# A three-part reordering in a one-core encoder layer: gates' chain, weight sums of the up-projection, places for the down weights

## The chip, the core and the metric

The kernel runs on one core of a Trainium2 chip. Its engines work side by side, each through its own row of instructions in a fixed order, and wait for one another by semaphores: TensorE does the matrix products (PE in the profile; its weight loads are PEld), VectorE (DVE) and ScalarE (ACT) the elementwise work, GpSimd (POOL) some sums, and SyncE (SP) issues most DMAs. The metric is the device time of one execution in microseconds (us); lower is better. TensorE's clock has two levels, 1.2 and 2.4 GHz, and the profile shows which of them was granted as a share of the full one.

## The reference, cut to what matters

One encoder layer over 1024 tokens of width 1024: a token mixer (a bidirectional mLSTM group and a neighbourhood attention group), cross-attention into 256 memory tokens, and a gated convolutional feed-forward block. The parts that the change touches are the mLSTM's gates and the two projections of the feed-forward block.

```python
# mLSTM, per chunk of 128 tokens: lfc = log_sigmoid(forget gate), ic = input gate
a = jnp.cumsum(lfc, axis=-1)
d_log = jnp.where(tril, a[..., :, None] - a[..., None, :] + ic[..., None, :], -jnp.inf)
m_t = jnp.maximum(a + m[..., None], jnp.max(d_log, axis=-1))
m_new = jnp.maximum(a_end + m, jnp.max(a_end[..., None] - a + ic, axis=-1))

# feed-forward: D_FF = 2816, so w_up is 1024 x 5632 and w_down 2816 x 1024
h = x @ w_up + b_up
h = lax.conv_general_dilated(h, w_dw[:, None, :], ...) + b_dw
g, u = jnp.split(h, 2, axis=-1)
y = jax.nn.gelu(g, approximate=False) * u
return y @ w_down + b_down
```

## The kernel before

All large products work on numbers split into a high and a low f16 half: ACT makes the high half (L204), DVE the low half (L205), and PE does three products for each (high by high L225, high by low L226, low by high L227). A split cannot start before its float32 source, the raw weights, has come by DMA, and it needs a place to write to. Places are rings: `wraw` has two raw places, `whi`/`wlo` five places each, `ur` two. Who asks for a place waits until the reader of its last holder is done.

The program is written in the order of the loops below, but a scheduler at build time sets each engine's final row, by its own estimate of times; generators (`next(...)`) and `issue_after` hints place the work of one stage between the products of another.

*Gates.* While the token columns are projected in four column blocks c of eight token tiles tt (the loop at L808, PE's `tk` products), the gates' chain `gate_gen` (L358) runs in six steps, each called by `next(gg)` at L835: the logarithms; the cumulative sums on PE (L376 to L378); a transpose of `g_sb` (L386) and 14 steps of a cumulative maximum on DVE (L394, L395, seven for each direction, alternating between two buffers `cx`) with the copies to `gm` (L399, L400); a product that turns the maxima into a row (L403) and the recursion over the chunks (L414, L416); the broadcast of it (L419 to L421); the last transpose (L432). Between them the splits of the next block's weights (`wlo<-wr`), copies out of PE's banks (`ev` L814, `stage` L205), statistics (`mx` L183, `l` L311) and, on POOL, sums for operands T (`tsum`, turned to f16 at L743) share DVE and POOL.

*Up-projection.* The work is divided into 22 units of w_up, and in each the 2x2 blocks of weights (A) and tokens (B) go through Winograd's form of Strassen's product: seven products with sums S1 to S4 of the weight blocks and T1 to T4 of the token blocks. `to_B` (L1315) turns a token tile into B, and every second one also makes its T sums on DVE (L1342 to L1345), in two `wraw` places, and splits them (ACT L1348, DVE or POOL L1349; `TX1l` and `TX1h` hold T). `Units.prep` makes a unit's S sums on POOL (L1505 to L1508), also in two `wraw` places, and then splits them on ACT and DVE. `units.load` (L1464) fetches a unit's raw weights into the `ur` ring, `units.bound` (L1471) takes their sum of absolutes, and `units.scale` a power of two from the maximum that PE's `mx` (L183) spreads. The start of it is written at L1524 to L1559. Before, `next(prep1)` (the S sums of the second unit) and `units.bound(2)` stood ahead of the loop that does the first products of both units and, in it, the last `to_B`.

*Down-projection.* The 1024 output columns are two halves c of 512, and the 22 rows of blocks f are in six groups j (four blocks in each, two in the last). `w_pair(j, c)` (L1650) loads and splits one such group. The first half runs over j outside and tiles tt inside (L1754), then over the last group j = 5 (L1771); the second half runs over the tiles (L1790), with j = 5 first and then j = 0 to 4. So the second half's first product needs the pair (5,1), and its first tile needs all six. Pair (5,1) has a place of its own in `yp`, before and after; before, all others used the `whi`/`wlo` ring, which still holds the first half's groups. Lines L1758 and L1774 copy and add the first half's results out of PE's banks (`half`).

Of the kernel before, what the change touches and what calls it, by code (L numbers as in the profile page):

```python
# [8 lines left out]
F32 = mybir.dt.float32  # L9
# [47 lines left out]
def encoder(ctx, tc, I, out):  # L57
# [21 lines left out]
    def bank(name):  # L79
        key = "mem" if name == "tk" else name  # L80
        turn[key] = turn.get(key, -1) + 1
        tag = SET[name][turn[key] % len(SET[name])]
        return pp.tile([128, 512], F32, name=name, tag=tag, bufs=NB[tag])
# [198 lines left out]
    with ExitStack() as ca:  # L282

        yml = None
        with ExitStack() as cm:
# [254 lines left out]
            with ExitStack() as c2:  # L540
# [257 lines left out]
                with ExitStack() as c1:  # L798
# [7 lines left out]
                    for c in range(4):  # L806
                        w, ic = cw[2 + c]
                        for tt in range(NT):  # L808
# [6 lines left out]
                            j = slice(c % 2 * 256, c % 2 * 256 + 256)  # L815
# [15 lines left out]
                                    next(cu0)  # L831
                            if c == 2 and tt == 4:
                                next(cu0)
                            if c < 2 and tt % 2 == 0:
                                next(gg, None)  # L835
                            if tt % 2:
                                with tc.issue_after(d.ins):
# [386 lines left out]
    with ExitStack() as cb_:  # L1224
# [3 lines left out]
        f16 = lambda t: t.bitcast(F16)  # L1228
# [210 lines left out]
        ur = cb_.enter_context(tc.tile_pool(name="unitraw", bufs=1, reuse_waits="tile"))  # L1439
# [104 lines left out]
        run(prep0)  # L1544
        units.load(2)
        next(o7)
        next(prep1)
        units.bound(2)

        with rtx:  # L1550

            X, Z, W = {}, {}, {}
            for v in range(2):
                X[v], Z[v] = bank("z"), bank("z")
                prod(X[v], v, "A11", "B11", True, False)
                if rq and v == 1:
                    to_B(*rq.pop(0))
                prod(Z[v], v, "A12", "B21", True, True)
                W[v] = bank("z")  # L1559

# [3 lines left out]
        with ExitStack() as cE:  # L1566
# [83 lines left out]
            def w_pair(j, c):  # L1650

                n = min(4, NFF - 4 * j)
                if j == 5 and c == 1:
                    h, l = yhome[5][:, 2, 0], yhome[5][:, 2, 1]
                else:
                    h, l = (wp.tile([128, 2048], F16, name=t, tag=t, bufs=5) for t in ("whi", "wlo"))
                for i in range(n // 2):
# [82 lines left out]
        with ExitStack() as cF:  # L1740
# [13 lines left out]
            for j in range(1, 5):  # L1754
                for tt in range(NT):
# [10 lines left out]
                        V.tensor_scalar(ratio, sy[1][0], s1, 2.0 ** -14, op0=OP.mult, op1=OP.mult)  # L1766
                    if j == 4 and tt == 0:
                        y_pair(NG, sy[1][1])
                    if j == 4 and tt in (4, 6):
                        w_pair((tt - 4) // 2, 1)  # L1770
            for tt in range(NT):  # L1771
                p2 = bank("dn")
                dmm(p2, tt, 0, range(NG, NFF), True, True)
                V.scalar_tensor_tensor(half0[:, tt], p2, ratio, half0[:, tt], op0=OP.mult, op1=OP.add)  # L1774
                if tt in (1, 3, 5):
                    w_pair(2 + tt // 2, 1)
            w_pair(5, 1)
            lb = yhome[5][:, 3].rearrange("p n t -> p (n t)").bitcast(F32)
            S.dma_start(lb, bcast_row(I["ln3_b"], D))
            rs = {}  # L1780
# [113 lines left out]
```

## Time and profile before

| | us |
|---|---|
| median of 3 runs | 1557.06 (1556.63 to 1559.12) |
| profiled execution, own time | 1562.55 |
| its span, first to last instruction | 1560.8 |
| PE busy in the span | 1476.6 (95%) |
| DVE, ACT, POOL busy | 1045.2, 807.2, 573.3 |
| mean granted clock of PE | 0.977 of full |

A row of a timeline gives the start and the length of an instruction (or of several in a run, with xN), and in square brackets how long its engine had been idle and what ended that. "dn<-whi,yp" reads: the instruction writes the tile dn and reads whi and yp. `z` are the up-projection's banks, `dn` the down-projection's, `tk` and `mem` those of the token projection. `yp` holds y (the input of the down-projection) in its halves. A step that PE waits for is found by its releaser; that one has a row on its own engine, with its own wait.

### The profile page before, as it was taken

The page shows a single profiled execution, that of the slowest core. Times are in us where ns is not written, and L with a number is a line of the kernel's source. Part 1 is how long each engine was busy: PE and PEld are TensorE (multiplying, and loading weights), DVE is VectorE, ACT ScalarE, POOL GpSimd, SP SyncE. Part 2 cuts the span into 40 slices and gives each one's busy share as a digit, 9 for nine tenths or more (in the row PEclk, how much of TensorE's full clock was granted, in tenths as well). Part 3 has the DMA queues.
Part 4 walks back from the last instruction along what each step waited for, and adds up shares of the span by engine and source line. Part 5 has one row for each costly group of instructions (what it writes and reads, how often), then busy time and mean ns, then how long its engine had stood idle before and what let it go on. Part 6 is the DMA issues. An engine that isn't in the chain of part 4 may idle for free.

```text
span 1560.8 us, 21755 instructions
## 1 busy us (share of the span) xinstructions
PE 1476.6 (95%) x8134; PEld 879.3 (56%) x8134; DVE 1045.2 (67%) x1961; ACT 807.2 (52%) x1367; POOL 573.3 (37%) x446
## 2 busy tenths in 40 slices
PE   7899899999999999999999979999999999997998
PEld 6788787456765888864555434444444444443443
DVE  7876756535667778575356768888888877925333
ACT  5444554655553666433344668777777756611000
POOL 6243265502324766043112364444444410301342
PEclk9999899999999999999999989999999999998999
DMA  8833564314644732653011332223223424832111
GB/s 297 323 139 122 173 204 157 111 48 130 162 136 149 229 125 82 243 189 122 28 41 41 122 138 109 108 108 116 114 109 122 169 87 157 296 112 69 41 68 54
DMA packets 84896, 208.62 MB, mean 134 GB/s; under 512 B 7091, under 2 KB 36019, under 8 KB 81462
## 3 DMA queue, kind: packets, MB, share of 16 engines
q1 hardware_dynamic: 84496, 206.46, 38.1%
q8 instruction: 64, 1.05, 0.3%
q0 software_dynamic: 144, 0.49, 0.2%
q14 instruction: 42, 0.34, 0.1%
q10 hardware_dynamic: 150, 0.27, 0.0%
HBM read 158.34 MB, written 49.35 MB: 133 GB/s over the span
## 4 chain that ended last, share of the span: by engine, by line
PE 52%; DVE 22%; DMA 9%; ACT 9%; issue 4%; POOL 4%; SPq 1%; DVEq 0%; ACTq 0%; POOLq 0%
PE dn L226 5%; PE dn L227 5%; PE dn L225 5%; PE S L225 3%; PE S L227 3%; PE S L226 3%; DMA sv<-in_w_down_dram 3%; DVE wlo L205 3%; DVE cbuf L1587 3%; DVE cbuf L1588 2%; PE z L226 2%; PE z L225 2%; PE z L227 2%; PE cl L225 2%; PE cl L226 2%
## 5 line engine op out<-in xcount | busy, mean ns | idle before, releaser
L225 PE MATMUL dn<-whi,yp 128*128 128x512 f16 x336 | 127.4, 382 | 1.4 <-ACT whi L204 1.4
L226 PE MATMUL dn<-wlo,yp 128*128 128x512 f16 x336 | 128.1, 382 | 0.0
L227 PE MATMUL dn<-whi,yp 128*128 128x512 f16 x336 | 127.9, 381 | 0.0
L1505 POOL TENSOR_TENSOR wraw<-ur 128x512 f32<-128x512 f32 x22 | 44.0, 2000 | 200.5 <-issue 186.4
L1587 DVE SCALAR_TENSOR_TENSOR cbuf<-C,wdw,cbuf 128x1024 f32<-128x1024 f32 x44 | 75.8, 1722 | 28.3 <-ACT cbuf L1586 28.2
L225 PEld LDWEIGHTS <-whi 128*128 128x128 f16 x540 | 53.6, 99 | 62.0 <-issue 9.5
L227 PEld LDWEIGHTS <-wlo 128*128 128x128 f16 x540 | 53.7, 99 | 59.6 <-DVE wlo L205 3.6
L226 PEld LDWEIGHTS <-whi 128*128 128x128 f16 x540 | 53.6, 99 | 57.3 <-issue 4.1
L205 DVE SCALAR_TENSOR_TENSOR wlo<-wraw,us,whi 128x1024 f16<-128x1024 f32 (+1 forms) x48 | 67.6, 1425 | 17.7 <-ACT whi L204 17.4
L253 ACT ACTIVATE r<-r,lnrs 128x1024 f32<-128x1024 f32 x19 | 23.6, 1243 | 99.6 <-DVE lnrs L252 99.6
L1588 DVE SCALAR_TENSOR_TENSOR cbuf<-C,wdw,cbuf 128x1024 f32<-128x1024 f32 x44 | 70.5, 1602 | 1.2
L225 PEld LDWEIGHTS <-yp 128*128 128x128 f16 x352 | 34.6, 98 | 51.9 <-issue 11.1
L204 ACT ACTIVATE whi<-wraw,us 128x1024 f16<-128x1024 f32 (+1 forms) x48 | 51.3, 1103 | 17.5 <-DVE us L177 11.3
L1586 ACT ACTIVATE cbuf<-C,bdw,wdw 128x1024 f32<-128x1024 f32 x44 | 54.5, 1238 | 10.6 <-DVE C L1623 9.8
L243 POOL TENSOR_TENSOR lnrs<-lnrs,mhalf 128x1 f32<-128x1 f32 x32 | 19.7, 616 | 105.6 <-DVE lnrs L242 90.2
L227 PEld LDWEIGHTS <-yp 128*128 128x128 f16 x352 | 34.7, 98 | 42.2 <-issue 1.1
L226 PEld LDWEIGHTS <-yp 128*128 128x128 f16 x352 | 34.6, 98 | 42.0 <-issue 1.1
L225 PE MATMUL tk<-whi,Be 128*128 128x256 f16 (+1 forms) x192 | 54.1, 282 | 1.4 <-ACT whi L204 1.4
L227 PE MATMUL tk<-whi,Be 128*128 128x256 f16 (+1 forms) x192 | 53.7, 280 | 0.0
L226 PE MATMUL tk<-wlo,Be 128*128 128x256 f16 (+1 forms) x192 | 53.6, 279 | 0.0
L225 PE MATMUL tk<-whi,Bo 128*128 128x256 f16 (+1 forms) x192 | 52.9, 275 | 0.0
L1182 ACT ACTIVATE P<-P,mn 128x256 f32<-128x256 f32 (+1 forms) x64 | 35.6, 557 | 33.3 <-DVE mn L1180 33.1
(496 smaller groups left out, 4863.2 us busy)
## 6 DMA issues: line engine op xcount, KB each, us to landing
ur<-in_w_up_dram SPq DMA_DIRECT2D x22, 1024.0 KB
sv<-in_w_down_dram SPq DMA_DIRECT2D x22, 512.0 KB
y<-cbuf SPq DMA_DIRECT2D x22, 512.0 KB
ur<-y SPq DMA_DIRECT2D x11, 1024.0 KB
wraw<-in_w_down_dram SPq DMA_DIRECT2D x22, 512.0 KB
r<-h SPq DMA_DIRECT2D x19, 512.0 KB
h<-r SPq DMA_DIRECT2D x16, 512.0 KB
wraw<-in_w_tok_dram SPq DMA_DIRECT2D x10, 512.0 KB
```

Source lines behind the costliest of these rows:

```text
L204: A.activation(hi, src, AF.Copy, scale=s)
L205: return V.scalar_tensor_tensor(lo, src, s, hi, op0=OP.mult, op1=OP.subtract)
L225: T.matmul(ps, lh, rh, start=first, stop=False, skip_group_check=skip)
L226: T.matmul(ps, lh, rl, start=False, stop=False, skip_group_check=skip)
L227: return T.matmul(ps, ll, rh, start=False, stop=last, skip_group_check=skip)
L243: G.tensor_tensor(rs[:, 0:1], rs[:, 0:1], mhalf[:, 0:1], OP.pow)
L253: A.activation(r, r, AF.Identity, scale=rs[:, 0:1], bias=rs[:, 1:2])
L1182: A.activation(P[:, :nk], P[:, :nk], AF.Exp, scale=-1.0, bias=mn[:, 0:1], accum_out=mn[:, 1:2])
L1505: G.tensor_tensor(S1, A21, A22, OP.add)
L1586: A.activation(c, C[:, 1:SEQ + 1], AF.Identity, scale=wdw[:, 1, j:j + 1], bias=bdw[:, j:j + 1])
L1587: V.scalar_tensor_tensor(c, C[:, 0:SEQ], wdw[:, 0, j:j + 1], c, op0=OP.mult, op1=OP.add)
L1588: V.scalar_tensor_tensor(c, C[:, 2:SEQ + 2], wdw[:, 2, j:j + 1], c, op0=OP.mult, op1=OP.add)
```

## The change

1. The gates' chain takes a step at every third tile, n = 8c + tt = 1, 4, 7, 10, 13, 16, where it took one at every second, n = 0, 2, 4, 6, 8, 10.
2. `next(prep1)` and `units.bound(2)` move behind the loop with the first products, so the last tile's `to_B` with its T sums comes ahead of the second unit's S sums.
3. The second half's down weights (3,1) and (4,1) go to places in the `ur` ring, each tile holding both halves. The pairs are called in the order (5,1), (0,1), (1,1), (2,1) at tt = 1, 3, 5, 7 of j = 4, and (3,1), (4,1) at tt = 0, 2 of the loop over the last group. Before, it was (0,1), (1,1) at tt = 4, 6 of j = 4, then (2,1), (3,1), (4,1) at tt = 1, 3, 5 of the next loop, and (5,1) behind it.

```diff
--- before.py
+++ after.py
@@ -831,7 +831,7 @@
                                     next(cu0)
                             if c == 2 and tt == 4:
                                 next(cu0)
-                            if c < 2 and tt % 2 == 0:
+                            if (8 * c + tt) % 3 == 1 and 8 * c + tt < 17:
                                 next(gg, None)
                             if tt % 2:
                                 with tc.issue_after(d.ins):
@@ -1544,8 +1544,6 @@
         run(prep0)
         units.load(2)
         next(o7)
-        next(prep1)
-        units.bound(2)
 
         with rtx:
 
@@ -1557,6 +1555,8 @@
                     to_B(*rq.pop(0))
                 prod(Z[v], v, "A12", "B21", True, True)
                 W[v] = bank("z")
+            next(prep1)
+            units.bound(2)
 
 
 
@@ -1652,6 +1652,9 @@
                 n = min(4, NFF - 4 * j)
                 if j == 5 and c == 1:
                     h, l = yhome[5][:, 2, 0], yhome[5][:, 2, 1]
+                elif j > 2 and c == 1:
+                    t = f16(ur.tile([128, 2048], F32, name="ur", tag="ur", bufs=2))
+                    h, l = t[:, :2048], t[:, 2048:]
                 else:
                     h, l = (wp.tile([128, 2048], F16, name=t, tag=t, bufs=5) for t in ("whi", "wlo"))
                 for i in range(n // 2):
@@ -1766,15 +1769,14 @@
                         V.tensor_scalar(ratio, sy[1][0], s1, 2.0 ** -14, op0=OP.mult, op1=OP.mult)
                     if j == 4 and tt == 0:
                         y_pair(NG, sy[1][1])
-                    if j == 4 and tt in (4, 6):
-                        w_pair((tt - 4) // 2, 1)
+                    if j == 4 and tt in (1, 3, 5, 7):
+                        w_pair((5, 0, 1, 2)[tt // 2], 1)
             for tt in range(NT):
                 p2 = bank("dn")
                 dmm(p2, tt, 0, range(NG, NFF), True, True)
                 V.scalar_tensor_tensor(half0[:, tt], p2, ratio, half0[:, tt], op0=OP.mult, op1=OP.add)
-                if tt in (1, 3, 5):
-                    w_pair(2 + tt // 2, 1)
-            w_pair(5, 1)
+                if tt in (0, 2):
+                    w_pair(3 + tt // 2, 1)
             lb = yhome[5][:, 3].rearrange("p n t -> p (n t)").bitcast(F32)
             S.dma_start(lb, bcast_row(I["ln3_b"], D))
             rs = {}
```

ACT's row at the end of the down-projection, before. Each `whi<-wraw` or `yp<-wraw` is half of a pair of down weights, the last two blocks alone being (5,c); `yp<-ur` are halves of y.

```order
L204 ACTIVATE whi<-wraw,sc 128x1024 x2
L204 ACTIVATE yp<-ur,sc 128x1024 x2
L204 ACTIVATE whi<-wraw,sc 128x1024 x7
L204 ACTIVATE yp<-ur,sc 128x1024 x2
L204 ACTIVATE whi<-wraw,sc 128x1024 x4
L204 ACTIVATE yp<-wraw,sc 128x1024
```

The same place after.

```order
L204 ACTIVATE whi<-wraw,sc 128x1024 x2
L204 ACTIVATE yp<-ur,sc 128x1024 x2
L204 ACTIVATE yp<-wraw,sc 128x1024
L204 ACTIVATE whi<-wraw,sc 128x1024 x7
L204 ACTIVATE ur<-wraw,sc 128x1024 x2
L204 ACTIVATE yp<-ur,sc 128x1024 x2
```

The single `yp<-wraw`, which is (5,1), has moved from the end to the front; (3,1) and (4,1) are now written to `ur`, one on either side of the last two blocks of y.

ACT's row at the start of the units, before (`unitYl` are the third unit's weights, `whi<-wraw,us` the second unit's S sums, L1348 the high halves of the T sums, L1611 the first results, L1630 a survey of w_down).

```order
L1348 ACTIVATE TX1l<-wraw 128x4x128
L1234 ACTIVATE r<-tp,wb_7277 128x128 x6
L1348 ACTIVATE TX1h<-wraw 128x4x128
L1348 ACTIVATE whi<-r 128x4x128
L204 ACTIVATE unitYl<-ur,us 128x1536
L204 ACTIVATE whi<-wraw,us 128x1024 x2
L1348 ACTIVATE TX1l<-wraw 128x4x128
L1348 ACTIVATE TX1h<-wraw 128x4x128
L1471 ACTIVATE whi,l_9397<-ur 128x2048
L1348 ACTIVATE TX1l<-wraw 128x4x128
L1630 ACTIVATE sv_9305,sums<-sv_9305 128x1024
L1348 ACTIVATE TX1h<-wraw 128x4x128
```

The same place after.

```order
L1348 ACTIVATE TX1h<-wraw 128x4x128
L1234 ACTIVATE r<-tp,wb_7277 128x128 x6
L1348 ACTIVATE TX1l<-wraw 128x4x128
L1348 ACTIVATE whi<-r 128x4x128
L1348 ACTIVATE TX1h<-wraw 128x4x128
L1348 ACTIVATE TX1l<-wraw 128x4x128
L1348 ACTIVATE TX1h<-wraw 128x4x128
L1611 ACTIVATE C_9307<-z,bup,us 128x4x128
L1611 ACTIVATE C_9309<-z,bup,us 128x4x128
L204 ACTIVATE unitYl<-ur,us 128x1536
L204 ACTIVATE whi<-wraw,us 128x1024
```

The five splits at L1348 of the last tile now stand together, ahead of the third unit's split; behind them come the first results and then the S sums' splits.

DVE's row in the gates' chain from the transpose's copy on (L390), before (`ev` are copies of `tk` banks, `wlo<-wr` low halves of the next block's weights, `l` a statistic).

```order
L390 COPY cx_1689<-s 64x128
L311 TENSOR_TENSOR l_1555<-l_1555 128x1
L394 TENSOR_TENSOR cx_1690<-cx_1689 32x128
L395 TENSOR_TENSOR cx_1690<-cx_1689 32x128
L394 TENSOR_TENSOR cx_1689<-cx_1690 32x128
L814 SCALAR_TENSOR_TENSOR ev<-tk,us,btok_1473 128x256
L395 TENSOR_TENSOR cx_1689<-cx_1690 32x128
L394 TENSOR_TENSOR cx_1690<-cx_1689 32x128
L395 TENSOR_TENSOR cx_1690<-cx_1689 32x128
L394 TENSOR_TENSOR cx_1689<-cx_1690 32x128
L395 TENSOR_TENSOR cx_1689<-cx_1690 32x128
```

The same place after.

```order
L390 COPY cx_1855<-s 64x128
L743 TENSOR_TENSOR TX1h<-tsum,TX1h 128x256
L743 TENSOR_TENSOR TX1l<-tsum,TX1l 128x256
L743 TENSOR_TENSOR TX1h<-tsum,TX1h 128x256
L394 TENSOR_TENSOR cx_1856<-cx_1855 32x128
L395 TENSOR_TENSOR cx_1856<-cx_1855 32x128
L814 SCALAR_TENSOR_TENSOR ev<-tk,us,btok_1473 128x256
L394 TENSOR_TENSOR cx_1855<-cx_1856 32x128
L395 TENSOR_TENSOR cx_1855<-cx_1856 32x128
L205 SCALAR_TENSOR_TENSOR wlo<-wr,sc,whi 128x1024
L394 TENSOR_TENSOR cx_1856<-cx_1855 32x128
L395 TENSOR_TENSOR cx_1856<-cx_1855 32x128
```

The cumulative maximum (L394, L395) is spread: a low half of weights now lies between its steps here and another one further on, and three splits of T sums (L743) ahead of it. On PE, in the order of before 77 products stand between the transpose L386 and the product L403, and 117 in the order of after.

## Rows read from the trace of the kernel before

**Rows 1.** Page of the profile: busy us of PE (share of the span), instructions.

```profile
PE 1476.6 (95%) x8134; PEld 879.3 (56%) x8134; DVE 1045.2 (67%) x1961; ACT 807.2 (52%) x1367; POOL 573.3 (37%) x446
```

**Rows 2.** PE's waits: engine line <- releaser: us in total, times, longest.

```profile
PE dn L225 <- ACT yp L204: 8.2, 1, 8.2
PE z L225 <- ACT TX1l L1348: 7.9, 1, 7.9
...
PE mx L183 <- DVE am L1472: 6.0, 14, 1.2
...
PE mem L225 <- DVE stage L205: 2.2, 1, 2.2
```

**Rows 3.** Timeline of PE: start us, us, instruction [idle before <-releaser].

```profile
1425.83 0.38 PE L226 MATMUL dn<-wlo,yp 128*128 128x512 f16 x1
...
1427.98 0.38 PE L227 MATMUL dn<-whi,yp 128*128 128x512 f16 x1
1436.54 0.59 PE L225 MATMUL dn<-yp 128*128 128x512 f16 x1 [8.18 <-ACT yp L204]
...
1441.52 0.38 PE L227 MATMUL dn<-whi,yp 128*128 128x512 f16 x1
```

**Rows 4.** Timeline of ACT, same columns, down-projection.

```profile
1397.15 2.19 ACT L204 ACTIVATE whi<-wraw,sc 128x1024 f16<-128x1024 f32 x2 [18.53 <-PE dn L227]
...
1428.45 2.19 ACT L204 ACTIVATE whi<-wraw,sc 128x1024 f16<-128x1024 f32 x2 [8.17 <-PE dn L227]
1435.34 1.15 ACT L204 ACTIVATE yp<-wraw,sc 128x1024 f16<-128x1024 f32 x1 [4.70 <-DMA wraw<-in_w_down_dram]
```

**Rows 5.** Chain that ended last, 1425 to 1450 us: start us, us, what.

```profile
1430.94 4.38 DMA wraw<-in_w_down_dram
```

**Rows 6.** Timeline of PE, start of the up-projection's units.

```profile
905.78 0.59 PE L225 MATMUL z<-TX1l,unitYh 128*128 128x512 f16 x1 [7.90 <-ACT TX1l L1348]
...
907.33 0.59 PE L226 MATMUL z<-TX1l,unitYh 128*128 128x512 f16 x1 [0.54 <-DVE TX1l L1349]
```

**Rows 7.** Timeline of ACT, start of the units.

```profile
904.06 1.15 ACT L204 ACTIVATE whi<-wraw,us 128x1024 f16<-128x1024 f32 x1 [4.31 <-POOL wraw L1508]
```

**Rows 8.** Timeline of POOL, start of the units.

```profile
899.16 2.67 POOL L1349 TENSOR_TENSOR wlo<-r,whi 128x512 f16<-128x512 f32 x1
901.79 2.24 POOL L1508 TENSOR_TENSOR wraw<-ur,wraw 128x512 f32<-128x512 f32 x1
```

**Rows 9.** Windows: us, busy us by engine (x instructions), PEclk, DMA share, GB/s.

```profile
160.00:165.00 5.00, 5.00 (x26) 3.46 (x24) 4.75 (x5) 3.44 (x7) 0.00 (x0) 0.52 0.32 108
165.00:170.00 5.00, 5.00 (x48) 4.48 (x47) 4.95 (x13) 1.20 (x3) 0.47 (x1) 1.00 0.63 168
905.00:910.00 5.00, 3.68 (x9) 1.24 (x9) 4.08 (x6) 2.38 (x4) 0.68 (x1) 0.50 0.93 360
```

**Rows 10.** Timeline of PE, gates' chain.

```profile
144.21 0.27 PE L386 MATMUL s<-ident,g_sb 128*64 128x128 f32 x1
...
158.93 0.37 PE L403 MATMUL s<-ident,gm 64*1 64x64 f32 x2 [4.05 <-DVE gm L400]
```

**Rows 11.** Timeline of DVE, gates' chain.

```profile
144.92 1.28 DVE L205 SCALAR_TENSOR_TENSOR wlo<-wr,sc,whi 128x1024 f16<-128x1024 f32 x1 [4.50 <-ACT whi L204]
...
155.44 0.72 DVE L394 TENSOR_TENSOR cx<-cx 32x128 f32<-32x128 f32 x1
156.19 0.28 DVE L395 TENSOR_TENSOR cx<-cx 32x128 f32<-32x128 f32 x1
```

**Rows 12.** Timeline of POOL, gates' chain.

```profile
155.35 0.67 POOL L739 TENSOR_TENSOR tsum<-tsum,Be 128x256 f32<-128x256 f32 x1
```

**Rows 13.** Groups by line, DVE, 149 to 159 us: busy us, mean ns.

```profile
L394 DVE TENSOR_TENSOR cx<-cx 32x128 f32<-32x128 f32 x7 | 3.6, 508 | 0.2
L395 DVE TENSOR_TENSOR cx<-cx 32x128 f32<-32x128 f32 x7 | 3.1, 449 | 0.2
```

**Rows 14.** Timeline of PE, from the units to the down-projection.

```profile
1308.63 0.59 PE L225 MATMUL z<-TX1h,unitA 128*128 128x512 f16 x1 [2.42 <-ACT C L1617]
```

## Prediction

> **What bounds the kernel now.** I read the page's busy table first, then PE's waits by line, then the timeline around each of the longest waits, and last the windows with the granted clock. The busy table [rows 1] shows TensorE (PE) busy 1476.6 us of the 1560.8 us span: some 84 us of idleness is all that a change of order can win, apart from time at the lower clock. The list of PE's waits [rows 2] shows that this idleness is not spread evenly. Two single events stand at its top: 8.2 us for a split on ScalarE (ACT) in the down-projection and 7.9 us for a split in the first units of the up-projection. The change touches these two stretches, and a third in which VectorE (DVE) works for the gates; each is a place with its own sum. (A split makes the high f16 half on ACT and the low half on DVE.) After each wait PE runs for a while at 1.2 instead of 2.4 GHz, and that belongs to the price of the wait.
>
> **Place 3, the second half's down weights (around 1428 us).** PE's timeline [rows 3] shows the whole loss: a product starts at 1427.98, the next at 1436.54, and until 1441.52 they start 0.43 us apart, where 0.215 us is the step at full rate (ten steps from 1425.83 to 1427.98). The wait costs 1436.54 − 1428.20 = 8.34 us. The half rate: twelve steps from 1436.54 to 1441.52, 4.98 us, where 12 × 0.215 = 2.58 us would do, 2.40 us. Together **10.7 us**.
>
> What ends last there is read from ACT [rows 4]. The split of pair (5,1), which PE needs first in the second half, stands last in ACT's row, at 1435.34. Ahead of it the pair (4,1) was split at 1428.45, released by PE: it waited 8.17 us for one of the five whi/wlo places, which came free only when PE's last product of the first half had read it. A raw place that (4,1) held was then refilled for (5,1), and that load, 4.38 us [rows 5], ended at 1435.3. Two splits and a load in a row make up the wait.
>
> After the change the order of ACT (quoted ahead) puts (5,1) before (5,0), and gives (3,1) and (4,1) places in the ur ring, whose loads are over. None of the three waits for a down product any more. Pair (2,1) still waits as in the row at 1397.15, for PE. Behind it come (3,1) and (4,1), each one load of 4.4 us and two splits of 2.2 us: some 7 us each, so 1397 + 2 + 7 + 7 = 1413 us even with no overlap, with the split of y blocks 20 and 21 (2.2 us by the same rows) between them, 1415 us. That is 13 us ahead of 1428, and (4,1) itself is read even later. On DVE the low halves now stand among the half-sum copies that empty PE's banks; the copies have the rest of that 13 us. So I take the whole 10.7 us; if a low half held a copy up, the loss would be one load, so the bound below is 10.7 − 4.4 = 6.3 us.
>
> **Place 2, the start of the units (875 to 912 us).** Before, PE has done the 48 products with B11 and B21 and waits from 897.9 to 905.78 for T1's high half on ACT, and again 0.54 us for its low half [rows 6]. ACT's row ahead of it is the split of the second unit's sums at 904.06, which had waited 4.31 us for POOL [rows 7]; the last of POOL's four sums ends at 904.03, and one low half of 2.67 us stands between them [rows 8]. The window from 905 to 910 has a granted clock of 0.50 and 9 products in 3.68 us of busy time [rows 9]; at 0.215 us 17 would have fitted, so 8 × 0.215 = 1.7 us went there. In all 7.9 + 0.5 + 1.7 = **10.1 us** are there to be won.
>
> The change lets the last token tile's T sums pass first, so S1·T1 and S2·T2 of unit 0 (24 products, 5.2 us) can start when the B products end. But the second unit's sums, their splits, and the third unit's scale now come afterwards, and PE reaches them early. In the order of after PE needs four things one after the other: T1's low half, unit 2's high split, the high split of the second unit's sums, and the low halves behind it. Each hangs on one more instruction of its chain. As a measure I take one split each, 1.15 us [rows 7]: 4 × 1.15 = 4.6 us of waits, and nothing for half rate. Gain 10.1 − 4.6, about **5.5 us**. The ends: all 10.1 us, if every chain is ahead of PE; and 10.1 − 4 × 2.67 = −0.6 us, if each piece is as long as the long low half on POOL [rows 8]. I stay nearer to the first since ACT's splits, not POOL's, end three of the four.
>
> **Place 1, the gates' chain (140 to 185 us).** Steps three and four are a transpose (L386, at 144.21) and the product with the maxima (L403, at 158.93): 14.7 us between them [rows 10], in which the order of before has 77 products, and at the end PE waited 4.05 us. Another wait nearby is 2.2 us for a bank's copy (stage L205) [rows 2]. From 160 to 165 us 26 products ran at a clock of 0.52 where 48 did in the next 5 us [rows 9]: 22/48 of 5 us = 2.3 us went to half rate. So 4.05 + 2.2 + 2.3 = **8.6 us** lie there.
>
> The change spreads the steps: in the order of after 117 products stand between L386 and L403. At 48 in 5 us they last 12.2 us. The chain itself gets no shorter: 14 maxima, and between them on DVE the copies of banks, two low halves of weights (wlo<-wr) and sums. Those low halves wait for loads, 4.5 us in the one row that shows it [rows 11]. If the chain takes the same 14.7 us as before, PE waits 2.5 us instead of 4.05 us; with about 1 us less at half rate I take **2.5 us**, and leave the wait for the copy as it is. The ends: all 8.6 us; and a chain with every maximum at 0.72 us (155.44 in the same rows), 14 × 0.72 = 10.1 us instead of 6.7, and one low half's wait of 4.5 us added, 22.6 us: PE would wait 10.4 us, a loss of 6.3 us.
>
> How long a maximum takes depends on what POOL does: 0.72 us at 155.44, while the last of POOL's sums for the T operands runs (to 156.02), and 0.28 us at 156.19 [rows 11, 12]. The fourteen together took 3.6 + 3.1 = 6.7 us [rows 13]. The Trainium skill, GPSIMD Engine Reference, section 1 (Specifications), gives a reason: GpSimd shares its SBUF interfaces with VectorE and contends with VectorE instructions that have two SBUF inputs. The maxima are such instructions, and the trace agrees. By that rule the chain's length is set by whether the next group of POOL's sums falls on it, and spreading the chain could as well move it away from them as onto them.
>
> **Elsewhere.** The new order also swaps neighbours at the passage from the units to the down-projection. There PE waited 2.42 us for C at a z product [rows 14]; in the order of after 12 such products come behind a group of down products, and that group needs low halves from DVE. I count **−1 us** (ends ±2.4, that wait). Nothing else in the order moves more than a few rows, and I count it at nothing; the units' loop is covered by PE itself, with 6.0 us of waits for a maximum in 14 events [rows 2].
>
> **Sum.** 10.7 + 5.5 + 2.5 − 1 = 17.7 us. The profiled execution took 1562.55 us (span 1560.8), 5.5 us above the median of the runs; it would come to 1544.9. The terms are taken off the median unchanged: 1557.06 − 17.7 = 1539.4, so **1539.5 us**, 1.1% faster.
>
> **Rivals.**
> - *The waits of places 1 and 2 move and do not shrink.* The chains there are long, and taking one thing forward puts another behind. For it: at place 2 four new waits can be named. Then place 3 is all: 10.7 − 1 = 9.7, 1547 us. Chance 0.20.
> - *POOL and the chain come apart.* If all maxima take 0.28 us, 14 × 0.28 = 3.9 us instead of 6.7 us, the chain is 11.9 us, below the 12.2 us of cover; L403 waits for nothing, 4.05 + 2.3 = 6.4 us instead of 2.5, and the time is 1535.5 us. (The Trainium skill's rule on the shared interfaces, named above, gives this where POOL is idle beside the chain.) Against it: POOL works for each column block, and a spread chain meets a block's sums sooner or later. Chance 0.10.
> - *Everything goes at all three places:* 10.7 + 10.1 + 8.6 = 29.4 us, 1527.5 us. Chance 0.07.
> - *The new places do not work:* the low halves in the ur ring hold up the bank copies on DVE, or (4,1) is late, and PE waits as long as before at the start of the second half. Only 5.5 + 2.5 − 1 = 7 us remain, 1550 us. The 13 us of room speak against it. Chance 0.06.
> - *Slower:* the second unit's sums now end later than 904.03, and with them the place for a later unit's raw weights comes free later. If the units' two-place ring hands that lag on, each of some 20 units makes PE wait longer for its maximum (am L1472). The waits there are 0.43 us in the mean and 1.2 us at the longest [rows 2]; 1.2 us more in each of 20 units is 24 us, 1557 − 17.7 + 24 = 1563 us. It decides from (17.7 + 3.1)/20 = 1.0 us per unit. The short waits of the loop speak against it: nothing there is that close to its end. Chance 0.02.
>
> **How the numbers follow.** The forecast has 0.55 with a band of its own from 1535 to 1544 us. The range 1531 to 1549 takes in the first two rivals and leaves out the other three, 0.15 in all. A measurement of this kernel can tell about 0.2%, 3.1 us, from no change. Faster by more than that: 0.95, since place 3 alone is three times as much; within: 0.03, if place 3 fails and place 1 or 2 turns bad; slower: 0.02.
>
> **What would show it.** Right: no wait above 1 us for a split of yp or whi between 1400 and 1450 us, and the granted clock at full rate there; ACT's (5,1) before 1365 us; at place 2 the 7.9 us replaced by several waits of 0.5 to 2 us; at place 1 a wait of 1 to 4 us left at L403. Wrong: a wait for ur or a half-sum copy at the start of the second half; at place 2 one wait above 4 us; at place 1 a wait for gm longer than 5 us; or longer waits for am through the units' loop.

## The result

Six runs of each on one chip: 1548.28 us in the median after the change (1545.48 to 1550.15), 1559.01 us before (1556.63 to 1564.65). The ratio is 0.9928, with a 95% interval from 0.9909 to 0.9947: the change makes the kernel faster by 0.72%, some 11 us (8 to 14). The prediction had said 1539.5 us, a gain of 17.7 us, with a range from 1531 to 1549.

The profiled execution after the change has a span of 1546.5 us, 14.3 us less than that of before. That is more than the runs show, since the profiled execution of before lay some 3 us above the median of its kernel. So differences between these two traces give the place of a gain, and the runs its size.

The page and PE's waits of the kernel after (engine, line, releaser: us in total, times, longest):

```profile
PE 1471.3 (95%) x8134; PEld 877.8 (57%) x8134; DVE 1053.5 (68%) x1961; ACT 811.2 (52%) x1369; POOL 573.3 (37%) x446
```

```profile
...
PE z L225 <- ACT C L1611: 5.7, 2, 5.3
PE mx L183 <- DVE am L1472: 4.6, 5, 1.5
...
PE tk L225 <- DVE stage L205: 3.3, 1, 3.3
...
PE dn L226 <- DVE wlo L205: 2.7, 1, 2.7
...
PE tk L225 <- DVE gm L399: 2.4, 1, 2.4
...
PE z L225 <- DVE C L1619: 2.1, 1, 2.1
```

Both waits at the top of [rows 2] are gone, that for yp and that for TX1l. A new one of 5.3 us has come, for a first result of the units (C, L1611), which the prediction does not name. The busy table says little of this: for the same 8134 instructions PE was busy 5.3 us less, while its mean granted clock was 0.983 after the change and 0.977 before.

**Where PE gained and gave back.** Products can be counted by the name of the tile that they write. The table sets the start of the n-th product into a tile in the two traces side by side; a negative difference is a lead of after. Among the z products PE's row is not the same in the two kernels, so there a row compares the same number of products and not always the same product.

| product | before, us | after, us | lead |
|---|---|---|---|
| 505th tk | 144.32 | 144.68 | +0.4 |
| 841st tk | 216.91 | 214.23 | −2.7 |
| 1st cu | 272.14 | 269.45 | −2.7 |
| 49th cu | 283.93 | 283.89 | −0.0 |
| 380th cl | 493.15 | 491.03 | −2.1 |
| 1st z | 881.04 | 878.19 | −2.9 |
| 73rd z | 914.71 | 901.82 | −12.9 |
| 217th z | 945.84 | 937.09 | −8.8 |
| 289th z | 961.44 | 960.66 | −0.8 |
| 1000th z | 1119.54 | 1115.81 | −3.7 |
| 1st dn | 1304.75 | 1300.71 | −4.0 |
| 400th dn | 1400.14 | 1396.59 | −3.6 |
| 700th dn | 1475.84 | 1461.56 | −14.3 |

Three places gained what they were meant to: 2.7 us at the gates, up to 10 us at the units' start, 10.7 us between the first and the second half of the down-projection. But the first lead was given back 60 us later, at the start of the cu products (most of it comes again before the 380th cl product, where the granted clock of before is 0.66 from 440 to 445 us and that of after is full; by the last section that may be chance), and the second one, whole, within 60 us: of 12.9 us at the 73rd z product 0.8 us are left at the 289th. A second execution of the kernel after, set beside the same trace of before, shows it too: 1.8 us of lead at the 1st z product, 8.9 us at the 145th, and 2.7 us behind at the 289th. Then the units' loop returns some 3 us in both executions of after (from 0.8 us ahead to 3.7 us ahead at the 1000th z product, and from 2.7 us behind to 0.4 us ahead), which is none of the three places.

**The down-projection.** ACT's timeline after (start us, us, instruction, idle before):

```profile
1358.13 1.15 ACT L204 ACTIVATE yp<-wraw,sc 128x1024 f16<-128x1024 f32 x1 [3.19 <-DMA wraw<-in_w_down_dram]
...
1393.55 2.19 ACT L204 ACTIVATE whi<-wraw,sc 128x1024 f16<-128x1024 f32 x2 [15.33 <-PE dn L227]
1400.37 1.15 ACT L204 ACTIVATE ur<-wraw,sc 128x1024 f16<-128x1024 f32 x1 [4.63 <-DMA wraw<-in_w_down_dram]
...
1409.32 2.19 ACT L204 ACTIVATE ur<-wraw,sc 128x1024 f16<-128x1024 f32 x2 [1.51 <-DVE yp L205]
```

This answers to [rows 4]: (5,1) is split at 1358, and the last pair at 1409 to 1411.5, in the first half's time. PE has no wait between 1380 and 1500 us.

**The units.** Three waits of up to 1 us stand where the long one was, then one of 2.1 us, and then the new one. PE's timeline after:

```profile
895.73 0.38 PE L226 MATMUL z<-TX1l,unitYh 128*128 128x512 f16 x1 [0.70 <-DVE TX1l L1349]
...
901.82 0.39 PE L225 MATMUL z<-Bh,unitYl 128*128 128x512 f16 x1 [0.96 <-ACT unitYl L204]
...
903.47 0.39 PE L225 MATMUL z<-TX1h,whi 128*128 128x512 f16 x1 [1.05 <-ACT whi L204]
...
934.51 0.38 PE L225 MATMUL z<-whi 128*128 128x512 f16 x1 [2.12 <-DVE C L1619]
...
955.59 0.59 PE L225 MATMUL z<-TX1h,whi 128*128 128x512 f16 x1 [5.32 <-ACT C L1611]
```

ACT's timeline at the end of that wait, after:

```profile
953.81 1.06 ACT L1591 ACTIVATE cbuf<-cbuf 128x1024 f32<-128x1024 f32 x1 [4.18 <-DVE cbuf L1588]
954.77 0.76 ACT L1611 ACTIVATE C<-z,bup,us 128x512 f32<-128x512 f32 x1
```

and the same two instructions before:

```profile
953.50 1.05 ACT L1591 ACTIVATE cbuf<-cbuf 128x1024 f32<-128x1024 f32 x1
954.44 0.77 ACT L1611 ACTIVATE C<-z,bup,us 128x512 f32<-128x512 f32 x1
```

This is the heart of the result. L1611 takes the first result of unit 3 out of PE's bank; PE goes on in that bank only then. It comes at 954.77 us after the change and at 954.44 us before, though PE had been 8.8 us ahead. ACT stood ready at 949.6 us and waited 4.18 us in front of the Gelu (L1591) of unit 1 for DVE's convolution (L1587, L1588, the two outer taps). PE had been brought forward; DVE had not. DVE began the convolution of unit 1 at 945.74 us, where before it was 946.28, and took longer. Its groups by line (busy us, mean ns) from 925 to 954 us after, and from 935 to 953 us before, each with the eight convolution steps of units 0 and 1:

```profile
L1587 DVE SCALAR_TENSOR_TENSOR cbuf<-C,wdw,cbuf 128x1024 f32<-128x1024 f32 x4 | 8.3, 2103 | 0.6 <-ACT cbuf L1586 0.6
L1588 DVE SCALAR_TENSOR_TENSOR cbuf<-C,wdw,cbuf 128x1024 f32<-128x1024 f32 x4 | 7.0, 1753 | 0.0
```

```profile
L1587 DVE SCALAR_TENSOR_TENSOR cbuf<-C,wdw,cbuf 128x1024 f32<-128x1024 f32 x4 | 5.1, 1282 | 1.6 <-ACT cbuf L1586 1.6
L1588 DVE SCALAR_TENSOR_TENSOR cbuf<-C,wdw,cbuf 128x1024 f32<-128x1024 f32 x4 | 5.1, 1280 | 0.1
```

10.2 us have become 15.3 us for the same work. Beside it POOL makes the S sums of later units: five of the eight steps, all beside a sum, take 2.2 to 2.3 us, a sixth 1.55 us, and the two that meet none 1.27 and 1.28 us; before, the convolutions fell in a gap of POOL from 933 to 955 us. POOL's timeline after (two of the sums that met them), and before, where the next sum follows an idle time of 22 us:

```profile
946.92 2.25 POOL L1507 TENSOR_TENSOR wraw<-ur 128x512 f32<-128x512 f32 x1
949.14 2.24 POOL L1508 TENSOR_TENSOR wraw<-ur,wraw 128x512 f32<-128x512 f32 x1
```

```profile
955.09 3.53 POOL L1505 TENSOR_TENSOR wraw<-ur 128x512 f32<-128x512 f32 x1 [22.01 <-issue]
```

It is the rule that the prediction weighed for the gates (the Trainium skill, GPSIMD Engine Reference, section 1, Specifications: GpSimd shares its SBUF interfaces with VectorE), and the trace agrees here too, with 2.2 to 2.3 us beside a sum against 1.28 us. The prediction looked for it at the gates, where it cost little (the fourteen maxima took 5.6 us after the change, 6.7 us before), and not at the units.

DVE's row is another one, too. After the change the low halves of a later unit stand ahead of unit 1's convolution, and before they stood behind it. DVE's timeline after, and before:

```profile
940.32 1.82 DVE L205 SCALAR_TENSOR_TENSOR unitYh<-ur,us,unitYh 128x1536 f16<-128x1536 f32 x1 [2.12 <-ACT unitYh L204]
...
945.74 2.30 DVE L1587 SCALAR_TENSOR_TENSOR cbuf<-C,wdw,cbuf 128x1024 f32<-128x1024 f32 x1
```

```profile
950.74 1.28 DVE L1588 SCALAR_TENSOR_TENSOR cbuf<-C,wdw,cbuf 128x1024 f32<-128x1024 f32 x1
951.94 1.81 DVE L205 SCALAR_TENSOR_TENSOR unitYh<-ur,us,unitYh 128x1536 f16<-128x1536 f32 x1
```

How much of the late end is owed to this order was not tried by itself.

### The profile page after: what moved, and what is told of

Read it like the earlier page. It is cut to its first block, busy times and chain, and to the rows that moved or that the text cites. A ratio compares the mean times of both kernels' runs of the same rounds, so it can differ in the third digit from the quotient of the medians.

```text
span 1546.5 us, 21750 instructions
## 1 busy us (share of the span) xinstructions
PE 1471.3 (95%) x8134; PEld 877.8 (57%) x8134; DVE 1053.5 (68%) x1961; ACT 811.2 (52%) x1369; POOL 573.3 (37%) x446
## 3 DMA queue, kind: packets, MB, share of 16 engines
q8 instruction: 64, 1.05, 0.3%
## 4 chain that ended last, share of the span: by engine, by line
PE 57%; DVE 21%; DMA 8%; ACT 8%; issue 4%; SPq 1%; POOL 1%; DVEq 0%; ACTq 0%; POOLq 0%
PE dn L226 5%; PE dn L227 5%; PE dn L225 5%; PE S L225 4%; PE S L227 4%; PE S L226 4%; DMA sv<-in_w_down_dram 3%; DVE cbuf L1587 3%; DVE cbuf L1588 3%; DVE wlo L205 2%; PE cl L225 2%; PE tk L225 2%; PE cl L227 2%; PE cl L226 2%; PE tk L227 2%
## 5 line engine op out<-in xcount | busy, mean ns | idle before, releaser
L226 PE MATMUL dn<-wlo,yp 128*128 128x512 f16 x272 | 103.3, 382 | 2.7 <-DVE wlo L205 2.7
L1587 DVE SCALAR_TENSOR_TENSOR cbuf<-C,wdw,cbuf 128x1024 f32<-128x1024 f32 x44 | 79.9, 1818 | 35.7 <-ACT cbuf L1586 35.7
L227 PE MATMUL dn<-whi,yp 128*128 128x512 f16 x272 | 103.5, 382 | 0.0
L225 PE MATMUL dn<-whi,yp 128*128 128x512 f16 x272 | 102.9, 382 | 0.5 <-ACT whi L204 0.5
L226 PEld LDWEIGHTS <-whi 128*128 128x128 f16 x540 | 53.3, 99 | 61.8 <-issue 9.4
L1588 DVE SCALAR_TENSOR_TENSOR cbuf<-C,wdw,cbuf 128x1024 f32<-128x1024 f32 x44 | 72.0, 1637 | 1.3
L226 PEld LDWEIGHTS <-yp 128*128 128x128 f16 x352 | 34.6, 98 | 41.9 <-issue 0.8
L226 PE MATMUL tk<-wlo,Be 128*128 128x256 f16 (+1 forms) x192 | 54.5, 285 | 0.0
```

The lines of the kernel that those rows point to most:

```text
L225: T.matmul(ps, lh, rh, start=first, stop=False, skip_group_check=skip)
L226: T.matmul(ps, lh, rl, start=False, stop=False, skip_group_check=skip)
L227: return T.matmul(ps, ll, rh, start=False, stop=last, skip_group_check=skip)
L1587: V.scalar_tensor_tensor(c, C[:, 0:SEQ], wdw[:, 0, j:j + 1], c, op0=OP.mult, op1=OP.add)
L1588: V.scalar_tensor_tensor(c, C[:, 2:SEQ + 2], wdw[:, 2, j:j + 1], c, op0=OP.mult, op1=OP.add)
```

## The experiments

Theory A on the whole: the down weights alone carry the gain; the lead at the units is lost again to a wait whose end is set by DVE's convolutions; the gates' lead is small. The first three kernels undo this into the three edits.

**Edit 1 alone.**

```diff
-                            if c < 2 and tt % 2 == 0:
+                            if (8 * c + tt) % 3 == 1 and 8 * c + tt < 17:
                                 next(gg, None)
```

> The kernel before with edit 1 alone (gates' steps at every third tile). Theory A (read from the trace of after): PE leads by 2.7 us at the end of the token products, 272 us, and gives it back at the start of the cu products, 277 to 284 us, so the time is 0 to 2 us below before. Rival B: the 2.7 us stay (and up to 1.9 us more around 440 us), 3 to 5 us below before.

Measured: 1553.99 us against 1560.54, ratio 0.9963 (0.9949 to 0.9978), 5.8 us (3.4 to 8.0). The trace shows what A says at the token products (3.1 us of lead at the first cu, 0.4 at the 49th), and yet the time fell more, by an amount nearer to B's, but not in B's way, since that lead did not stay. In the pair of traces some 3 us come in the units' loop (the lead is 0.9 us at the 289th z and 4.3 us at the first dn), where PE's waits for maxima (am L1472) sum to 2.9 us between 960 and 1300 us instead of 6.0 us:

```profile
PE mx L183 <- DVE am L1472: 1.5, 5, 0.4
PE z L225 <- DVE am L1472: 1.4, 3, 0.6
```

The edit's lines do not touch the loop, but the scheduler built another row for it. Matched by the names of what they write and read, 98 of PE's 1548 instructions between 960 and 1300 us of before stand at least 12 places from where they stood; with edit 3 alone, and with the gates' steps one tile later (below), none has moved at all. So this run is not the gates alone, and its 5.8 us can't be put down to them. Why the scheduler chose another row was not tried. The profiled execution, 1557.69 us, also lies 3.7 us above this kernel's median, so its trace need not show all of the gain.

**Edit 2 alone.** The two lines `next(prep1)` and `units.bound(2)` are moved as in the change.

> The kernel before with edit 2 alone (the last tile's T sums ahead of the second unit's S sums). Theory A: PE leads by about 8.7 us at 925 us, and loses it around 935 and 955 us to waits for the first results of units 2 and 3 (L1611, L1619), so the time is within 2 us of before. Rival B: that loss belongs to something else in the kernel after, such as the earlier start of the stage, and some 5 us or more of the lead stay.

Measured: 1557.56 us, ratio 0.9982 (0.9970 to 0.9993), 2.8 us (1.1 to 4.7). Between the two, nearer to A, though the interval reaches 4.7 us: in the trace PE wins 8.1 us from the first to the 49th z product, and of these 2.2 us are left at the 289th. The waits for L1611 are here 14.6 us in 10 events, eight of them, 9.3 us, in the loop after 960 us.

**Edit 3 alone**, the three hunks in `w_pair` and the loops of the down-projection.

> The kernel before with edit 3 alone (second half's down weights). Theory A: the wait of 8.2 us at 1428 us and the half rate behind it go, 10.7 us below before, the whole of what the kernel after wins but a remainder of 0 to 2 us. Rival B: the three edits share the gain, and this one gives 6 to 8 us.

Measured: 1551.10 us, ratio 0.9936 (0.9923 to 0.9949), 10.0 us (8 to 12). Theory A. In the trace PE gains 10.7 us from the 400th to the 700th dn product, the term of the sum to a tenth.

**Edit 3 without its places**: the order of calls is that of the change, the pairs (3,1) and (4,1) still go to the `whi`/`wlo` ring.

```diff
-                elif j > 2 and c == 1:
-                    t = f16(ur.tile([128, 2048], F32, name="ur", tag="ur", bufs=2))
-                    h, l = t[:, :2048], t[:, 2048:]
```

> The kernel before with the order of calls of edit 3, (5,1) first and (3,1), (4,1) last, but no places in the ur ring: all but (5,1) still use the five whi/wlo places. Theory A: the order does nearly all, since what now waits for the last place, (4,1), is needed last; its raw weights are there, so its splits come some 3 us behind the last product of the first half, 9 us ahead of their first use; 8 to 11 us below before, as e_down. Rival B: the places are needed; PE waits 4 us or more in the second half's first tile and the gain is under 6 us.

Measured: 1550.74 us, ratio 0.9943 (0.9925 to 0.9961), 8.9 us (6 to 12), about as much as with the places (10.0 us). Theory A. The last pair still waits for PE, in ACT's timeline of this kernel:

```profile
1429.05 2.19 ACT L204 ACTIVATE whi<-wraw,sc 128x1024 f16<-128x1024 f32 x2 [8.17 <-PE dn L227]
```

but PE has no wait between 1395 and 1460 us: the pair is (4,1) now, which the second half reads last of six, and its raw weights are there. The same wait of ACT cost 10.7 us in front of (5,1), and costs nothing in front of (4,1). It was the order that paid; the places of their own were not needed here.

**The gates' steps one tile later, but as dense as before.**

```diff
-                            if c < 2 and tt % 2 == 0:
+                            if c < 2 and tt % 2 == 1:
                                 next(gg, None)
```

> The kernel before with the gates' steps at n = 1, 3, 5, 7, 9, 11, so one tile later than before, but as dense. Theory A: edit 1 gains by putting more products between the steps; with the same density the wait for gm at L403 stays at 3 us or more and the time is within 2 us of before. Rival B: what counts is the place of the steps against the loads and POOL's sums; the time moves by 3 us or more either way.

Measured: 1557.91 us against 1559.56, ratio 0.9988 (0.9973 to 1.0002): no difference that can be told, as theory A has it for the time. But the trace speaks against theory A's mechanism. The wait for gm at L403 has gone altogether; PE's waits from 130 to 200 us in this kernel, and in the kernel after:

```profile
PE tk L225 <- DVE ev L814: 1.7, 1, 1.7
PE mem L227 <- DVE wlo L205: 1.3, 3, 0.7
PE mx L183 <- DVE l L311: 1.0, 1, 1.0
PE tk L225 <- DVE stage L205: 0.9, 1, 0.9
```

```profile
PE tk L225 <- DVE stage L205: 3.3, 1, 3.3
PE tk L225 <- DVE gm L399: 2.4, 1, 2.4
PE mx L183 <- DVE l L311: 0.4, 1, 0.4
```

PE leads by 7.7 us at the first cu product here, and by 2.7 us in the kernel after. So in these traces the place of the steps at the gates, against loads and sums, counts more than their distance. Of these 7.7 us, 4.4 are left at the 49th z product, and the runs show less still, by the 3 us that the trace of before stands too high.

**The Gelu of unit 1 behind the first result of unit 3.** In `post`, what follows the convolutions is a function of its own, called for unit 1 after `take(3, "C11")` (cut):

```diff
-                cg, cu = cs
+                return cs
+
+            def post_b(v):
+
+                cg, cu = (cbuf[:, 2 * (v % 2) + a] for a in range(2))
                 A.activation(cg, cg, AF.Gelu)
...
                 take(v, "C11")
+                if v > 1 and (v - 2) == 1:
+                    post_b(v - 2)
...
                     post(v - 1)
+                    if not (v - 1) == 1:
+                        post_b(v - 1)
```

> The kernel after, with the Gelu of unit 1 and what follows it (L1591 to L1594) written behind the first result of unit 3 (L1611), so that the copy that PE waits for 5.3 us does not stand behind the Gelu on ACT. Theory A: the place of L1611 in ACT's row is what takes the lead back; the 5.3 us wait and the half rate behind it go, 6 to 8 us below the kernel after (17 to 19 us below before). Rival B: ACT and DVE have too much to do in this stretch whatever the order; another wait takes the place, and the time is within 2 us of the kernel after (9 to 13 us below before).

Measured: 1545.83 us, ratio 0.9905 (0.9892 to 0.9917), 2 to 4 us below the kernel after in the medians, though the intervals overlap. Theory A fell in this form. ACT's order is as wanted, but the wait is 4.4 us still, and ACT's row shows why (L1615 is L1611 of after):

```profile
952.82 0.78 ACT L1615 ACTIVATE C<-z,bup,us 128x512 f32<-128x512 f32 x1 [4.10 <-DVE cbuf L1588]
```

The first result itself waits for the convolution. It is written into a C tile, of which there are four, two for each of two units, and unit 3's is the one that unit 1's convolution reads. So ACT's order was one of two ties between DVE and PE; the C tiles are the other.

**Six C tiles.** The next four were run on one chip: the kernel after again, six C tiles alone, six with the later Gelu, and a kernel without POOL's sums.

```diff
-            Cs = [wk.tile([128, SEQ + 2], F32, name=f"C{i}") for i in range(4)]
+            Cs = [wk.tile([128, SEQ + 2], F32, name=f"C{i}") for i in range(6)]
...
-                    C, j = Cs[2 * (v % 2) + a], a * NFF + v
+                    C, j = Cs[2 * (v % 3) + a], a * NFF + v
```

(and `Cg, Cu` in the same way.)

> The kernel after, unchanged, beside the next three on one chip: some 11 us below before (9 to 13 us). If the sum of the three edits alone were right (5.8 + 2.8 + 10 us), it would be 17 to 19 us below.

> The kernel after with six C tiles alone; the Gelu of unit 1 still stands ahead of the first result of unit 3 on ACT. Theory A: since the Gelu waits for the same convolution, the wait of some 5 us stays and the time is within 2 us of after. Rival B: the time falls by 4 us or more, the scheduler's order being another with more tiles.

> late_gelu_1 with six C tiles where there are four, so that the first result of unit 3 (L1615 here, L1611 in after) waits neither for the Gelu of unit 1 on ACT nor, through its C tile, for the convolution of unit 1 on DVE. Theory A (the C tile hands DVE's backlog on to PE): the wait of 4.4 us at 953 us and the half rate behind it go, 5 to 8 us below late_gelu_1. Rival B (ACT and DVE have too much to do in this stretch): another wait takes the place within the next two units, within 2 us of late_gelu_1.

Measured, against 1559.8 us of before: the kernel after 1546.63 us, ratio 0.9925 (0.9910 to 0.9940). Six tiles alone 1534.61 us, 0.9842 (0.9829 to 0.9854). Six tiles and the later Gelu 1534.64 us, 0.9840 (0.9827 to 0.9852). Theory A on the C tiles holds: 12 us below the kernel after, and some 10 us below the later Gelu alone, where 5 to 8 had been said. That the Gelu would keep the wait in `cs3` was wrong: with the tile free, the scheduler itself puts the first result ahead of the Gelu, which still waits for DVE but with nobody behind it. ACT's timeline of `cs3`:

```profile
943.90 0.77 ACT L1611 ACTIVATE C<-z,bup,us 128x512 f32<-128x512 f32 x1
948.58 1.06 ACT L1591 ACTIVATE cbuf<-cbuf 128x1024 f32<-128x1024 f32 x1 [3.90 <-DVE cbuf L1588]
```

PE's lead on the trace of before is 12.4 us at the 145th z product and 12.4 us at the 289th, where the kernel after has fallen from 11.6 to 0.8. DVE is only a little faster for it: the eight convolution steps of units 0 and 1 still take 13.7 us in `cs3` (7.4 us at L1587 and 6.3 us at L1588), but PE no longer waits for them. In the units behind it up to 4.8 us of that lead are given back (waits of 0.4 to 1.1 us stand there), and most of it comes again in the loop. The later Gelu adds nothing once the tiles are there. `cs3` beats both kernels, by 1.6% and 0.8%. Six tiles in the kernel before were not run, so what they are worth without the three edits isn't shown.

**Is it POOL beside DVE?** In `prep`, units 3 and 4 split the raw weights instead of the sums.

> The kernel after with POOL's S sums of units 3 and 4 left out (their splits read the raw weights instead, so the result of these two units is another). Theory C (DVE's convolutions of units 0 and 1 take 2.2 us in place of 1.28 us because POOL sums beside them): the convolutions between 925 and 955 us take 1.28 us each, the wait of 5.3 us shrinks to under 2 us, and the time is 4 to 8 us below after. Rival D (the amount of DVE's work, not POOL beside it): the wait stays above 4 us and the time is within 2 us of after.

Measured: 1546.66 us, ratio 0.9916 (0.9902 to 0.9930), the same as the kernel after (0.9925). At the place theory C holds. DVE's groups by line from 945 to 956 us (L1595 and L1596 are the two convolutions here, the four steps of unit 1) show 1.28 us each:

```profile
L1596 DVE SCALAR_TENSOR_TENSOR cbuf<-C,wdw,cbuf 128x1024 f32<-128x1024 f32 x2 | 2.6, 1285 | 0.0
L1595 DVE SCALAR_TENSOR_TENSOR cbuf<-C,wdw,cbuf 128x1024 f32<-128x1024 f32 x2 | 2.6, 1279 | 0.0
```

and no wait above 1.4 us is left from 920 to 975 us. (Of unit 0's four steps one still takes 1.63 us, beside a sum for another unit.) But the whole did not gain, and here rival D has the time. In the trace this kernel has 16 waits for C of about 1 us in the units (8.3 us for L1619 and 6.9 us for L1625, its numbers of L1611 and L1617), and PE's lead of 3.0 us at the 289th z product is 4.7 us of lag at the first dn. That execution took 1552.43 us, 6 us above the kernel's median, and PE's row in the loop is another one too, so where a typical execution loses the gain is not shown. POOL beside DVE makes the one long wait; taking it away did not make the kernel faster. That the four C tiles are the reason is likely by `cs3`, but no run combines six tiles with the sums left out.

**What edit 2 is worth with six tiles.** `cs3` with edit 2 taken back:

> The kernel cs3 with edit 2 taken back (edits 1 and 3 and six C tiles). Theory A: with six tiles the lead that edit 2 gives at 905 us is kept, so taking edit 2 back costs 6 to 10 us against cs3. Rival B: six tiles help by themselves wherever the stage starts, and edit 2 is worth no more than the 3 us that it gave alone.

Measured: 1540.09 us, ratio 0.9878 (0.9854 to 0.9902) against 0.9842 for `cs3`: some 5.6 us (1 to 10 by the two intervals), between the two theories. The runs alone can't tell it from the 2.8 us that the edit gave by itself; the traces can: from the first z product to the 289th PE gains 7.7 us with edit 2 and 1.4 us without it. That it comes so near to the 5.5 us of the prediction's place 2 is chance, since the terms there were other ones.

**The later Gelu for every unit, with six tiles.**

> cs3 with the Gelu and what follows it written behind the first result of the unit two later, for every unit. Theory A: in cs3 the loop's remaining waits for C (0.9 us at 956 and 974 us) come from ACT's order; they go and 2 to 4 us are won. Rival B: the loop is bound by PE and by what ACT and DVE do in all; within 2 us of cs3.

Measured: 1537.26 us, ratio 0.9856 (0.9831 to 0.9882); no gain on `cs3`. Rival B, as far as runs on two chips can be compared.

## Why the prediction was right, and where its size was off

It was right in sign, in what carries the gain, and the time lies in the range, at its upper end. The sum said 17.7 us; 11 were measured. The time missed the forecast's own band (1535 to 1544 us) and came out at 1548.3 us, next to the 1547 us of the first rival, which had a chance of 0.20. Most of its signs of being right came; so did one of the signs of being wrong, a single wait above 4 us in the units, but at 955 us, some 40 us behind the stretch that it had worked out.

- **Place 3, 10.7 us:** 10.0 us alone (8 to 12), 10.7 us in the traces. Each step held. Only the credit was wrong: the places in the ur ring, on which much of the working rests, were not needed; the order alone does it.
- **Place 2, 5.5 us:** the step that failed. At the place itself the prediction was even too low: three of the four waits that it names came, 0.70, 0.96 and 1.05 us, where 1.15 us each had been taken for four, and PE won 8.8 us from the first z product to the 145th. What failed is what was said of the rest: "I count it at nothing; the units' loop is covered by PE itself". In the kernel after that holds only behind the first result of unit 3. Ahead of it the wait of 7.9 us had given DVE time; with that gone, DVE's convolutions end last, and two ties, the C tiles and ACT's order, hand it on to PE in waits of 2.1 and 5.3 us. In the trace of after the lead at the 289th z product is 0.8 us, where it was 2.9 us at the first: together with the others the edit won nothing up to there. Alone it gave 2.8 us; with the C tiles' tie off it is worth some 5.6 us. The first rival (waits that move and do not shrink) is what happened, but 50 us further on and with an engine that it didn't name.
- **Place 1, 2.5 us:** 2.7 us in the trace at the end of the token products, and 2.39 us of wait for gm where 2.5 were said (it stands at a tk product, nine instructions ahead of L403). That is partly luck: the chain took not 14.7 us but 20.9 us (158.65 to 179.59). Of these 15.3 us passed under products, where 12.2 had been worked out (the granted clock was 0.72 from 160 to 165 us), and a wait of 3.3 us for stage copies, which stood behind low halves of weights on DVE, fell inside and delayed L403 itself. The lead was then given back at the cu products. The run of edit 1 alone shows 5.8 us, but with another row for the units' loop; the run that moves the gates' steps by one tile and leaves the loop's row as it was shows no difference that can be told.
- **"Nothing else in the order moves more than a few rows":** this reading was wrong. In the trace of after 81 of PE's 1548 instructions between 960 and 1300 us stand at least 12 places from where they stood before, matched as above. The sum has that at nothing; in both traces of after the loop returns some 3 us, and no run tells how much of it comes from the other row.
- **From the units to the down-projection, −1 us:** a wait of 2.7 us for a low half (L226 dn), with 0.5 us ahead of it, in place of the 2.42 us of [rows 14] and 1.4 us ahead of it; the lead is 3.4 us at the 1600th z product and 3.6 us at the 400th dn. So it is nothing, where −1 was said, and inside its bounds.
- **The edits do not add up.** 5.8 + 2.8 + 10.0 = 18.6 us alone against 11 or 12 us together (0.9928 and 0.9925). The difference, some 7 us, is more than the interval of any one of them. It isn't that edits 1 and 2 both bring PE forward to the same stretch: with edit 1 alone PE comes to the first z product 0.6 us later than in the trace of before. What edit 1 alone gained came behind that, in a loop with a row of its own, and the kernel after has yet another row there. How much of it is lost together with edit 2 stays open; no run tells it apart.

## What to carry to other kernels

When a wait of one engine is removed, ask of the engines that had been catching up in it: their backlog, and not the next wait in the list, may be what comes last. A lead is only kept if there are buffers to hold it; two more tiles, on top of the three edits, were worth as much here as the edits together. Where a scheduler sets the rows, compare the built rows of a stretch that an edit should leave alone before its time is put down to the edit. And before buffers are added for a late load, look at the order in which what waits is used: the same wait costs all or nothing by who stands behind it.

## What the runs showed of the hardware beyond that

The same wait is followed by the lower clock in one execution and not in another. At the start of the cu products two executions of the kernel after waited 2.22 and 2.21 us for the same low half; the windows around (us, busy us by engine with the number of instructions, PEclk, DMA share, GB/s) show half rate behind the first

```profile
275.00:280.00 5.00, 2.78 (x10) 1.02 (x9) 4.38 (x6) 1.47 (x3) 2.36 (x3) 0.83 0.78 269
280.00:285.00 5.00, 5.00 (x21) 2.10 (x20) 0.73 (x1) 3.85 (x8) 4.13 (x4) 0.83 0.03 11
```

and none behind the second:

```profile
275.00:280.00 5.00, 3.25 (x15) 1.49 (x16) 3.68 (x5) 2.16 (x4) 2.35 (x2) 1.00 0.70 237
280.00:285.00 5.00, 5.00 (x26) 2.49 (x25) 0.79 (x3) 3.12 (x7) 3.89 (x4) 1.00 0.02 5
```

Ten products fewer in ten us, some 2 us of time; from the first cu product to the 49th it was 14.4 and 12.7 us. So a wait of about 2 us cost here 2 us, or nearly 4 with the half rate behind it, in executions of one and the same kernel, and a lead of that size in one pair of traces, as at 284 us in the table, isn't evidence for an edit.
